# An encoder block on one core: sum of q or k first in a unit's side work, and feed-forward values without the token's scale

## The chip, the cores and the metric

The kernel runs on one core of one Trainium2 chip. The metric is the device time of one launch in microseconds (us), lower is better. Before the change it is 940.92 us, the median of three runs that lie between 940.85 and 941.05.

The core's engines are named as in its profile: PE (TensorE, matrix products), PEld (the loading of PE's weights, which overlaps with PE), DVE (VectorE), ACT (ScalarE), POOL (GpSimd) and SP (SyncE, which here only issues DMA transfers). Each takes its instructions in the order in which the program gives them. SBUF is the core's main on-chip memory, PSUM the memory that PE writes its sums to.

## The reference, cut to what matters

One encoder layer on 256 tokens of width 2048, all in float32. `D_FF` is 5504 (43 tiles of 128), there are 12 query heads of width 128 in 4 groups of three that share one key and value head.

```python
h = rmsnorm(x, norm1_g)                      # x / sqrt(mean(x*x) + EPS) * g, per token
q, k, v, u = split(h @ w_in)                 # widths 1536, 512, 512, 512
# window attention, per query head:
scores = q @ k.T * HEAD_DIM**-0.5 - slope * abs(t - s)      # only |t - s| <= 128
m = max(scores.max(-1), sink)
p = exp(scores - m); p = p / (p.sum(-1) + exp(sink - m))
a = rmsnorm(p @ v, attn_out_g)
f = rmsnorm(real(fft2(u per group)) @ w_fourier, fourier_out_g)
x = x + concat(a, f) @ w_out
h = rmsnorm(x, norm2_g)
gate, val = split(h @ w_up)                  # 5504 columns each
gate = conv over 3 tokens, per column, + dw_b
x = x + (gelu(gate) * val) @ w_down
y = rmsnorm(x, normf_g)
```

Each token's norm is one number for the token (the scale, `1/sqrt(mean + EPS)`) and one per column (`g`). The scale of a token can therefore be applied behind a product with a weight matrix as well as ahead of it.

## The kernel before

**Two halves of a float32.** PE multiplies in a rounded form of float32 (`fp32r`). Each operand is kept as a `hi` half (rounded, a copy on ACT) and a `lo` half (what the rounding lost, a subtraction on DVE), and a product is the sum of three: hi by hi, hi by lo, lo by hi. So all weights are split on the way: `split` (lines 174 to 184) takes a raw weight tile of 128 x 2048 (1 MB), ACT writes `hi` (L181), DVE writes `lo` (L182). A split costs each of them about two microseconds.

**Units.** The work up to the feed-forward part is a row of 40 units, each with one such weight tile: 0 to 3 for u, 4 to 7 for v, 8 to 23 for k and q (`QK_ORDER`: a key head, then its three query heads, four times over), 24 to 39 for the output projection. Raw tiles are loaded on SP's queue three units ahead, in a ring of three; they are split two units ahead. A unit (`unit`) runs in this order: the list `before` of that unit (matmuls of other work), its own matmuls (`still_weights`, recorded as L350), the list `beside`, then `step` with the split of the unit two later, then the list `behind`. The order of all instructions is written out by these lists; no scheduler moves anything. So the order within `beside` is the order in which ACT, DVE, POOL and SP meet the pieces of work.

**The head work.** Attention is laid beside the matmuls of the q and k units and of the first eight output units. A query head whose unit is n passes through these stages:

- n+1, `qk_out`: ACT copies one half of the PSUM sum (L631), DVE adds the other half (L633), for a key also times the token's scale. Then `qk_parts` makes the two halves: ACT `hi`, DVE `lo`, for a query at L269 and L270 (in `split_scaled`), for a key at L643 and L644.
- n+2, `scores` (six matmuls, L654, in `before`, so ahead of the unit's own) and `scores_out`: two DVE instructions add the distance term and take the maxima `mx` (L670), and two tiny POOL instructions on 128 x 2 make `neg` from them (L674, L675). In `behind`, after the split, `exps`: two exponentials on ACT with `neg` as the bias (L684), one for the sink (L688), a tiny POOL sum.
- n+3, `weigh`: reciprocal and two DVE multiplications (L697). For heads 0 to 9 (`FLIPS`) `flip_out` follows: a 32 by 32 transpose on DVE (L314) and four DMAs on SP. Heads 10 and 11 are turned by PE one unit later instead (`turn`, `turn_out`: ACT L716, DVE L717).
- n+4, `flip_in`: one DMA on SP. n+6, `flip_parts`: the halves of the turned weights, two ACT (L739) and two DVE (L740) instructions.
- n+7 (for heads 10 and 11 n+5), `values` (six matmuls, L749, in `before`) and `values_out`, which squares the result on ACT (L486), makes its halves (L269, L270) and adds the squares up on POOL (L490).

In any one q unit, several heads are thus under way, each at another stage. The order within `beside` is set in the loop over `i` below `slot_of`: `flip_parts`, `weigh` with `flip_out`, `flip_in`, `qk_out`, `values_out`, `turn_out`, `scores_out`, `qk_parts`, and after these the split.

**The feed-forward part.** 43 gate tiles and 43 value tiles, each one weight tile; `scaled_sum` copies one half of the PSUM sum (ACT, L922), adds the other (DVE, L924) and multiplies by `r2b`, the token's scale spread over all partitions (DVE, L925). The gate goes through the convolution (`gate_conv`) and GELU, then `val_mult` multiplies it with the value tile. The down-projection of the first 36 tiles is done in five groups by a scheme with seven products in place of eight for a matrix of two by two blocks (`product` items); their results are added onto `xs`, the residual stream x, by `product_out` (L1122) as they come, or held in PSUM or in `Z` and added at the end by `shared_out`. Tiles 36 to 39 (`LATE`) and 40 to 42 (`LAST`) are multiplied plainly; `last_post` adds the last of them and starts the squares of the final norm, with `EPS` added for the first piece (lines 1170 to 1172).

Of the kernel before, what the change touches and what calls it, by code (L numbers as in the profile page):

```python
# [8 lines left out]
F32 = mybir.dt.float32  # L9
F32R = mybir.dt.float32r  # L10
AF = mybir.ActivationFunctionType
ALU = mybir.AluOpType

P = 128
D = 2048
# [11 lines left out]
EPS = 1e-6  # L27
# [28 lines left out]
FLIPS = range(NH - 2)  # L56
# [48 lines left out]
def block_kernel(  # L105
# [19 lines left out]
    nc = tc.nc  # L125
    SL = slopes()
    ctx.enter_context(tc.manual_schedule())
    base = ctx.enter_context(tc.tile_pool(name="base", bufs=1))
# [131 lines left out]
    ps = bank(dn, "ps_warm")  # L260
# [13 lines left out]
    def rstd_of(ssq, width, name, n=2, r=None):  # L274

        var = base.tile([P, n], F32, tag="var" + name, name="var" + name)
        nc.vector.tensor_scalar(var, ssq, 1.0 / width, EPS, ALU.mult, ALU.add)
        if r is None:
            r = base.tile([P, n], F32, tag="rstd" + name, name="rstd" + name)
        nc.gpsimd.tensor_tensor(r, var, half_pow[:, 0:n], ALU.pow)  # L280
        return r
# [7 lines left out]
    def spread(r, dst, name):  # L289

        t = wp.tile([P, 512], F32, tag="junk", name=f"diag{name}")
        dgs = [t[:, b * P : (b + 1) * P] for b in range(2)]
        for b, dg in enumerate(dgs):
            nc.vector.tensor_scalar(dg, ident, r[:, b : b + 1], None, ALU.mult)
        ps = bank(dn, "ps_spread" + name)
        for b in range(2):
            nc.tensor.matmul(
                ps[:, b * P : (b + 1) * P], ones, dgs[b], start=True, stop=True
            )
        nc.vector.tensor_copy(dst, ps[:, :S])  # L300
# [72 lines left out]
    before, beside, behind = {}, {}, {}  # L373

    def at(when, i, f, *a):
        when.setdefault(i, []).append((f, a))
# [13 lines left out]
    for c in range(4):  # L390
        t = base.tile([P, 4, 512], F32R, tag=f"hT{c}", name=f"hT{c}")
# [234 lines left out]
    qk_sb, st = {}, {}  # L626
    sq_a = ph.tile([P, S], F32, tag="sq", name="sq_a")

    def qk_out(kind, h, ps):
        tmp = ph.tile([P, S], F32, tag="tmp", name=f"tmp_{kind}{h}", bufs=2)  # L630
        nc.scalar.activation(tmp, ps[:, S : 2 * S], AF.Copy)  # L631
        add = ph.tile([P, S], F32, tag="add", name=f"add_{kind}{h}", bufs=2)
        nc.vector.tensor_tensor(add, ps[:, 0:S], tmp, ALU.add)  # L633
        if kind == "k":
            nc.vector.tensor_tensor(add, add, r1b, ALU.mult)
        st["add", kind, h] = add
# [125 lines left out]
    for i in range(N_QK, N_OUT + 8):  # L762
        heads = {i - s: h for (kind, h), s in slot_of.items() if kind == "q"}
        new = [kh for kh, s in slot_of.items() if i - s == 1]
        for n, h in sorted(heads.items()):
            if n == 5 + 2 * (h in FLIPS):
                at(before, i, values, h)
        if 4 in heads and heads[4] not in FLIPS:
            at(before, i, turn, heads[4])
        if 2 in heads:  # L770
            at(before, i, scores, heads[2])
        if 6 in heads and heads[6] in FLIPS:
            at(beside, i, flip_parts, heads[6])
        if 3 in heads:
            at(beside, i, weigh, heads[3])
            if heads[3] in FLIPS:
                at(beside, i, flip_out, heads[3])
        if 4 in heads and heads[4] in FLIPS:
            at(beside, i, flip_in, heads[4])
        for kind, h in new:  # L780
            at(beside, i, lambda k=kind, h=h: qk_out(k, h, st.pop(("ps", k, h))))
        for n, h in sorted(heads.items()):
            if n == 5 + 2 * (h in FLIPS):
                at(beside, i, values_out, h)
        if 4 in heads and heads[4] not in FLIPS:
            at(beside, i, turn_out, heads[4])
        if 2 in heads:
            at(beside, i, scores_out, heads[2])
        for kind, h in new:
            at(beside, i, qk_parts, kind, h)  # L790
        if 2 in heads:
            at(behind, i, exps, heads[2])

# [126 lines left out]
    def scaled_sum(ps, name):  # L920
        tmp = fp.tile([P, S], F32, tag="ftmp", name=f"ft_{name}")
        nc.scalar.activation(tmp, ps[:, S : 2 * S], AF.Copy)  # L922
        add = fp.tile([P, S], F32, tag="fadd", name=f"fa_{name}", bufs=3)
        nc.vector.tensor_tensor(add, ps[:, 0:S], tmp, ALU.add)  # L924
        nc.vector.tensor_tensor(add, add, r2b, ALU.mult)  # L925
        sums_of[name] = add

    def gate_conv(j):
# [182 lines left out]
    def product_out(g, c, p, ps):  # L1111
        tt = nc.vector.tensor_tensor
        if p in ("P6", "P7"):
            z = Z[c, p]
            if g == 0:
                nc.scalar.activation(z, ps, AF.Copy)
            else:
                tt(z, ps, z, ALU.add)
        else:
            n, t = {"P2": (0, 0), "N3": (1, 0), "N4": (0, 1)}[p]  # L1120
            xb = xs[2 * n + c][:, t, :]
            tt(xb, ps, xb, ALU.add)  # L1122

    def shared_out(c, step):

        p1, n5, u, p7 = held[c, "P1"], held[c, "N5"], Z[c, "P6"], Z[c, "P7"]
        x00, x10, x01, x11 = (xs[2 * n + c][:, t, :] for n in range(2) for t in range(2))
        tt = nc.vector.tensor_tensor
        if step == 0:
            tt(u, p1, u, ALU.add)  # L1130
            tt(x00, p1, x00, ALU.add)
            w = st["w", c] = wp.tile([P, 512], F32, tag="junk", name=f"sum01_{c}")
            tt(w, n5, u, ALU.subtract)
        elif step == 1:
            tt(u, u, p7, ALU.add)
            tt(x01, x01, st["w", c], ALU.add)
            tt(x10, x10, u, ALU.add)
        else:
            w = st.pop(("w", c))
            tt(w, w, p7, ALU.subtract)  # L1140
            tt(x11, x11, w, ALU.add)

    def by_parts(ps, o, hi, lo, n, first, last):

# [14 lines left out]
    def last_post(c, b, ps, o=0, n=512):  # L1159

        xb = xs[c][:, b, o : o + n]
        nc.vector.tensor_tensor(xb, ps, xb, ALU.add)
        if c == 3:
            return
        junk = wp.tile([P, 512], F32, tag="junk", name=f"junkc{c}{b}")
        nc.scalar.activation(
            junk, xb, AF.Square, scale=D**-0.5, accum_out=ssq3[:, b, c : c + 1]
        )
        if c == 0:
            nc.vector.tensor_scalar(  # L1170
                ssq3[:, b, 3:4], ssq3[:, b, 0:1], EPS, None, ALU.add
            )
        if (c, b) == (1, 1):
            nc.gpsimd.tensor_tensor(
                ssq3[:, b, 3:4], ssq3[:, b, 3:4], ssq3[:, b, 1:2], ALU.add
            )
        if (c, b) not in ((1, 1), (2, 1)):
            nc.gpsimd.tensor_tensor(xb, xb, gfb[:, c * 512 : (c + 1) * 512], ALU.mult)
# [44 lines left out]
        still_weights(hi, lo, ps, range(12, NK))  # L1223
    tot2 = base.tile([P, 2], F32, tag="tot2", name="tot2")
    nc.vector.tensor_reduce(tot2, ssq2, mybir.AxisListType.X, ALU.add)
    spread(rstd_of(tot2, D, "2"), r2b, "2")
    ff_step(1)
    up_posts(1, *items[0], pair[0][0])
    up_posts(2, *items[1], pair[1][0])
# [208 lines left out]
```

## Time and profile before

The profiled execution took 941.03 us on the device; its span, from the first to the last recorded instruction, is 938.9 us. The mean granted clock of TensorE was 0.997 of full speed.

| engine | busy us | share of the span | instructions |
|---|---|---|---|
| PE | 928.0 | 99% | 5005 |
| PEld | 803.5 | 86% | 5005 |
| DVE | 765.5 | 82% | 945 |
| ACT | 539.6 | 57% | 672 |
| POOL | 72.9 | 8% | 104 |

The DMA queues moved 223.25 MB, 238 GB/s on average. The head work lies between about 70 and 200 us of the span, the feed-forward part from about 250 us to the end.

How to read the rows: a row of the order of time begins with its start (us from the start of the span) and its duration, then engine, line, operation, what it writes and reads, shapes, and the count of equal instructions that follow on one another; in brackets the idle time ahead of it and the instruction that ended it. A row of a group begins with the line, has the count behind an x, and then the group's busy time in us and the mean of one in ns. `lo<-raw,hi` is the DVE part of a split and thus marks the pace of the units. PE's busy share stands near 99% because a matmul's record is pipelined with the next one's; where PE waits, its next row says for how long and for what.

### The profile page before, as it was taken

The page shows a single profiled execution, that of the slowest core. Times are in us where ns is not written, and L with a number is a line of the kernel's source. Part 1 is how long each engine was busy: PE and PEld are TensorE (multiplying, and loading weights), DVE is VectorE, ACT ScalarE, POOL GpSimd, SP SyncE. Part 2 cuts the span into 40 slices and gives each one's busy share as a digit, 9 for nine tenths or more (in the row PEclk, how much of TensorE's full clock was granted, in tenths as well). Part 3 has the DMA queues.
Part 4 walks back from the last instruction along what each step waited for, and adds up shares of the span by engine and source line. Part 5 has one row for each costly group of instructions (what it writes and reads, how often), then busy time and mean ns, then how long its engine had stood idle before and what let it go on. Part 6 is the DMA issues. An engine that isn't in the chain of part 4 may idle for free.

```text
span 938.9 us, 12849 instructions
## 1 busy us (share of the span) xinstructions
PE 928.0 (99%) x5005; PEld 803.5 (86%) x5005; DVE 765.5 (82%) x945; ACT 539.6 (57%) x672; POOL 72.9 (8%) x104
## 2 busy tenths in 40 slices
PE   9999999999999999999999999999999999999996
PEld 7888888888888888888888888888888888888885
DVE  7657888778677777798888997878979789989986
ACT  7755666645554555566555665556655556655553
POOL 0102222300000000000000000000000000000002
PEclk9999999999999999999999999999999999999998
DMA  9965767557757668887797778777787978779652
GB/s 367 309 224 169 231 196 236 193 174 281 243 221 232 177 227 238 278 269 239 220 296 252 246 216 286 237 262 232 260 248 240 309 224 269 241 233 273 194 179 90
DMA packets 55148, 223.25 MB, mean 238 GB/s; under 512 B 21136, under 2 KB 25744, under 8 KB 31536
## 3 DMA queue, kind: packets, MB, share of 16 engines
q1 hardware_dynamic: 50544, 192.94, 56.8%
q0 software_dynamic: 4544, 29.49, 16.9%
q8 instruction: 39, 0.64, 0.3%
q14 instruction: 21, 0.17, 0.1%
HBM read 216.13 MB, written 6.29 MB: 237 GB/s over the span
## 4 chain that ended last, share of the span: by engine, by line
PE 95%; DVE 2%; ACT 1%; issue 1%; DMA 0%; POOL 0%; DVEq 0%; POOLq 0%; ACTq 0%
PE ps_val L350 25%; PE ps_gate L350 25%; PE ps_q L350 5%; PE ps_P L1148 3%; PE ps_P L1149 3%; PE ps_P L1147 3%; PE ps_N L1148 3%; PE ps_N L1149 3%; PE ps_N L1147 3%; PE ps_k L350 2%; PE ps_a L333 2%; PE ps_a L335 2%; PE ps_a L334 2%; PE ps_s L654 1%; PE ps_ff L333 1%; PE ps_ff L335 1%
## 5 line engine op out<-in xcount | busy, mean ns | idle before, releaser
L182 DVE TENSOR_TENSOR lo<-raw,hi 128x2048 fp32r<-128x2048 f32 (+1 forms) x129 | 293.5, 2275 | 53.9 <-ACT hi L181 53.6
L181 ACT ACTIVATE hi<-raw 128x2048 fp32r<-128x2048 f32 (+1 forms) x129 | 245.3, 1902 | 36.7 <-PE ps_a L334 14.6
L350 PE MATMUL ps_val<-hU,hi 128*128 128x512 f32 x688 | 236.2, 389 | 0.0
L350 PE MATMUL ps_gate<-hU,hi 128*128 128x512 f32 x688 | 236.2, 389 | 0.0
L350 PE MATMUL ps_val<-hU,lo 128*128 128x256 f32 x688 | 189.9, 276 | 0.0
L350 PE MATMUL ps_gate<-hU,lo 128*128 128x256 f32 x688 | 189.9, 276 | 0.0
L350 PEld LDWEIGHTS ps_gate<-hU,hi 128*128 128x128 f32 x688 | 129.1, 188 | 26.8
L350 PEld LDWEIGHTS ps_val<-hU,hi 128*128 128x128 f32 x688 | 129.1, 188 | 26.8
L350 PEld LDWEIGHTS ps_gate<-hU,lo 128*128 128x128 f32 x688 | 129.1, 188 | 1.3
L350 PEld LDWEIGHTS ps_val<-hU,lo 128*128 128x128 f32 x688 | 129.1, 188 | 1.3
L922 ACT ACTIVATE ft_g<-ps_gate 128x256 f32<-128x256 f32 x43 | 16.5, 384 | 123.0 <-PE ps_gate L350 123.0
L922 ACT ACTIVATE ft_v<-ps_val 128x256 f32<-128x256 f32 x43 | 16.5, 384 | 91.5 <-PE ps_val L350 91.5
L350 PE MATMUL ps_q<-hT,hi 128*128 128x512 f32 x192 | 65.1, 391 | 0.0
L1147 PE MATMUL ps_P<-hi_P,op_P 128*128 128x512 f32 x144 | 56.0, 389 | 0.0
L1148 PE MATMUL ps_P<-hi_P,op_P 128*128 128x512 f32 x144 | 56.0, 389 | 0.0
L1149 PE MATMUL ps_P<-lo_P,op_P 128*128 128x512 f32 x144 | 56.0, 389 | 0.0
L350 PE MATMUL ps_q<-hT,lo 128*128 128x256 f32 x192 | 51.2, 277 | 0.0
L1039 DVE TENSOR_TENSOR lo_N<-sumw,hi_N 128x2048 fp32r<-128x2048 f32 (+1 forms) x20 | 41.5, 2077 | 9.4 <-ACT hi_N L1038 9.2
L1147 PE MATMUL ps_N<-hi_N,op_N 128*128 128x512 f32 x108 | 42.0, 389 | 0.0
L1148 PE MATMUL ps_N<-hi_N,op_N 128*128 128x512 f32 x108 | 42.0, 389 | 0.0
L1149 PE MATMUL ps_N<-lo_N,op_N 128*128 128x512 f32 x108 | 42.0, 389 | 0.0
L350 PEld LDWEIGHTS ps_q<-hT,hi 128*128 128x128 f32 x192 | 35.2, 188 | 6.6
(389 smaller groups left out, 1598.9 us busy)
## 6 DMA issues: line engine op xcount, KB each, us to landing
raw<-in_w_up SPq DMA_DIRECT2D x86, 1024.0 KB, 5.6
raw<-in_w_in SPq DMA_DIRECT2D x20, 1024.0 KB, 5.3
raw<-in_w_out SPq DMA_DIRECT2D x16, 1024.0 KB, 4.9
sumw<-in_w_down POOLq DMA_DIRECT2D x16, 1024.0 KB, 8.7
raw<-in_w_down_late SPq DMA_DIRECT2D x4, 1024.0 KB, 7.0
raw<-in_w_down_last SPq DMA_DIRECT2D x4, 768.0 KB, 4.2
turnp<-flip SPq DMA_DIRECT2D x40, 64.0 KB, 2.9
flop<-turnp SPq DMA_DIRECT2D x10, 256.0 KB, 4.7
```

Of the source, the lines that this page charges most:

```text
L181: nc.scalar.activation(hi[:, 0:n], raw[:, 0:n], AF.Copy)
L182: nc.vector.tensor_tensor(lo[:, 0:n], raw[:, 0:n], f32(hi[:, 0:n]), ALU.subtract)
L333: nc.tensor.matmul(ps, ah, wh, start=first and q == q0, stop=False)
L334: nc.tensor.matmul(ps, al, wh, start=False, stop=False)
L335: nc.tensor.matmul(ps, ah, wl, start=False, stop=last and q == q0 + len(kk) - 1)
L350: nc.tensor.matmul(ps[:, x], (hi, lo)[i][:, k * P : (k + 1) * P], hk(k)[:, x], start=n == 0 and k == 0, stop=n == len(order) - 1 and k == ...
L654: nc.tensor.matmul(ps[:, b * S : (b + 1) * S], qT[:, qo + b * P : qo + (b + 1) * P], kT[:, ko : ko + S], start=n == 0, stop=n == 2,)
L922: nc.scalar.activation(tmp, ps[:, S : 2 * S], AF.Copy)
L1039: nc.vector.tensor_tensor(lo, src, f32(hi), ALU.subtract)
L1147: nc.tensor.matmul(ps, o[:, 0, p, :], hi[:, s], start=first and p == 0, stop=False)
L1148: nc.tensor.matmul(ps, o[:, 1, p, :], hi[:, s], start=False, stop=False)
L1149: nc.tensor.matmul(ps, o[:, 0, p, :], lo[:, s], start=False, stop=last and p == n - 1)
```

## The change

Four things are done.

1. In the loop that fills the lists, the order within `beside` becomes: `qk_out`, `flip_parts`, `qk_parts`, `values_out`, `weigh` with `flip_out`, `flip_in` or `turn_out`, `scores_out`. The sum of q or k, which stood in the middle, now comes first; the parts of q or k, which stood last, come third; `scores_out` now stands last, directly ahead of the split.
2. `scaled_sum` multiplies by the token's scale for gate tiles only. The value tiles stay without it, so what the down-projection adds up is too large by `1/scale` per token.
3. To match, x is divided by the token's scale before the down-projection's results are added onto it: `rms2` is the reciprocal of the scale, and the first addition onto each block of `xs` becomes `x * rms2 + value` in one instruction with a scalar per partition (in `product_out` for the first group, in `shared_out` for the block that is only touched there).
4. The final norm then works on x divided by the scale. It is the same if its `EPS` is divided by the square of the scale: `eps3 = EPS * rms2 * rms2` takes the place of `EPS` in `last_post`. `rms2` and `eps3` are two new tiles of 128 x 2 in the pool `base`, made once by three DVE instructions.

```diff
@@ the loop over i that fills the lists
+        for kind, h in new:
+            at(beside, i, lambda k=kind, h=h: qk_out(k, h, st.pop(("ps", k, h))))
         if 6 in heads and heads[6] in FLIPS:
             at(beside, i, flip_parts, heads[6])
+        for kind, h in new:
+            at(beside, i, qk_parts, kind, h)
+        for n, h in sorted(heads.items()):
+            if n == 5 + 2 * (h in FLIPS):
+                at(beside, i, values_out, h)
         if 3 in heads:
             at(beside, i, weigh, heads[3])
             if heads[3] in FLIPS:
                 at(beside, i, flip_out, heads[3])
-        if 4 in heads and heads[4] in FLIPS:
-            at(beside, i, flip_in, heads[4])
-        for kind, h in new:
-            at(beside, i, lambda k=kind, h=h: qk_out(k, h, st.pop(("ps", k, h))))
-        for n, h in sorted(heads.items()):
-            if n == 5 + 2 * (h in FLIPS):
-                at(beside, i, values_out, h)
-        if 4 in heads and heads[4] not in FLIPS:
-            at(beside, i, turn_out, heads[4])
+        if 4 in heads:
+            at(beside, i, flip_in if heads[4] in FLIPS else turn_out, heads[4])
         if 2 in heads:
             at(beside, i, scores_out, heads[2])
-        for kind, h in new:
-            at(beside, i, qk_parts, kind, h)
         if 2 in heads:
             at(behind, i, exps, heads[2])
@@ scaled_sum
-        nc.vector.tensor_tensor(add, add, r2b, ALU.mult)
+        if name[0] == "g":
+            nc.vector.tensor_tensor(add, add, r2b, ALU.mult)
@@ product_out
-            tt(xb, ps, xb, ALU.add)
+            if g == 0:
+                nc.vector.scalar_tensor_tensor(xb, xb, rms2[:, t : t + 1], ps, ALU.mult, ALU.add)
+            else:
+                tt(xb, ps, xb, ALU.add)
@@ shared_out
-            tt(x11, x11, w, ALU.add)
+            nc.vector.scalar_tensor_tensor(x11, x11, rms2[:, 1:2], w, ALU.mult, ALU.add)
@@ last_post
-                ssq3[:, b, 3:4], ssq3[:, b, 0:1], EPS, None, ALU.add
+                ssq3[:, b, 3:4], ssq3[:, b, 0:1], eps3[:, b : b + 1], None, ALU.add
@@ ahead of the feed-forward items
-    spread(rstd_of(tot2, D, "2"), r2b, "2")
+    r2 = rstd_of(tot2, D, "2")
+    spread(r2, r2b, "2")
+    rms2 = base.tile([P, 2], F32, tag="rms2", name="rms2")
+    eps3 = base.tile([P, 2], F32, tag="eps3", name="eps3")
+    nc.vector.reciprocal(rms2, r2)
+    nc.vector.tensor_tensor(eps3, rms2, rms2, ALU.mult)
+    nc.vector.tensor_scalar(eps3, eps3, EPS, None, ALU.mult)
```

## The prediction

> **What bounds the kernel now.** I read the stretches of the span first, then PE's order of time where the head work runs, then DVE, POOL and ACT in the same place. In the stretches (time, PE busy, PEld, DVE, ACT, POOL, clock, DMA share, GB/s) the feed-forward part is one unbroken run of matmuls.
>
> ```profile
> 264.00:845.00 581.00, 581.00 (x3197) 505.70 (x3196) 493.93 (x533) 335.57 (x347) 23.54 (x28) 1.00 0.78 247
> ```
>
> PE is busy 581.00 of 581.00 us and DVE leaves 87 us idle. What DVE saves there shortens nothing. Now PE in order of time: the last matmuls of a q unit, the scores, the next unit.
>
> ```profile
> 77.14 0.40 PE L350 MATMUL ps_q<-hT,lo 128*128 128x256 f32 x2
> ...
> 78.09 0.40 PE L350 MATMUL ps_k<-hT,hi 128*128 128x512 f32 x1
> ...
> 95.44 0.40 PE L350 MATMUL ps_q<-hT,lo 128*128 128x256 f32 x2
> ...
> 96.78 0.39 PE L350 MATMUL ps_q<-hT,hi 128*128 128x512 f32 x1
> ...
> 122.00 0.40 PE L350 MATMUL ps_q<-hT,lo 128*128 128x256 f32 x2
> ...
> 123.97 0.40 PE L350 MATMUL ps_q<-hT,hi 128*128 128x512 f32 x1
> ...
> 149.18 0.40 PE L350 MATMUL ps_q<-hT,lo 128*128 128x256 f32 x2
> ...
> 151.47 0.39 PE L350 MATMUL ps_q<-hT,hi 128*128 128x512 f32 x1
> ```
>
> From the first row to the last an undisturbed passage takes 0.95 us (77.14 to 78.09). The others take 1.34, 1.97 and 2.29: PE loses 0.39, 1.02 and 1.34, together 2.75 us, waiting for the parts of q. That is all the first edit can win. The three places are heads 3, 6 and 9; I call them s3, s6 and s9.
>
> Why is q late? DVE's splits (L182) mark one unit each:
>
> ```profile
> 90.97 2.29 DVE L182 TENSOR_TENSOR lo<-raw,hi 128x2048 fp32r<-128x2048 f32 x1 [1.26 <-ACT hi L181]
> ...
> 95.71 0.42 DVE L270 SCALAR_TENSOR_TENSOR qT<-add_q,qT 128x256 fp32r<-128x256 f32 x1 [0.48 <-ACT qT L269]
> ...
> 117.93 2.29 DVE L182 TENSOR_TENSOR lo<-raw,hi 128x2048 fp32r<-128x2048 f32 x1 [0.87 <-ACT hi L181]
> ...
> 124.72 2.29 DVE L182 TENSOR_TENSOR lo<-raw,hi 128x2048 fp32r<-128x2048 f32 x1 [1.38 <-ACT hi L181]
> ...
> 130.31 2.29 DVE L182 TENSOR_TENSOR lo<-raw,hi 128x2048 fp32r<-128x2048 f32 x1 [1.27 <-ACT hi L181]
> ...
> 137.63 2.29 DVE L182 TENSOR_TENSOR lo<-raw,hi 128x2048 fp32r<-128x2048 f32 x1 [0.88 <-ACT hi L181]
> 139.84 0.75 DVE L740 TENSOR_TENSOR pt<-flop,pt 128x256 fp32r<-128x256 f32 x2
> ...
> 140.70 0.90 DVE L697 TENSOR_SCALAR sc<-sc,ex 128x256 f32<-128x256 f32 x2
> ...
> 145.41 2.29 DVE L182 TENSOR_TENSOR lo<-raw,hi 128x2048 fp32r<-128x2048 f32 x1 [0.87 <-ACT hi L181]
> ...
> 149.54 0.38 DVE L633 TENSOR_TENSOR add_q<-ps_q,tmp_q 128x256 f32<-128x256 f32 x1
> ...
> 150.40 0.42 DVE L270 SCALAR_TENSOR_TENSOR qT<-add_q,qT 128x256 fp32r<-128x256 f32 x1
> ```
>
> Four units (6.79, 5.59, 7.32, 7.78) make a group of 27.48 us, as long as PE takes from s6 to s9 (123.97 to 151.47: 27.50, of which 1.34 is the wait). So this loop of DVE and ACT sets the pace here, not PE. In each unit DVE waits about 0.9 to 1.4 us for ACT's hi half, because ACT waits for the sum of q or k first.
>
> **The change part by part.** *The order of side work.* The sum comes ahead of the weighting and the stream transpose, so ACT's hi half starts sooner and that wait shrinks. But q's or k's lo half no longer stands between the scores' maxima and the split. In before, one unit late in the stage already has no q or k work and so has the new order:
>
> ```profile
> 144.28 0.31 POOL L674 TENSOR_TENSOR neg<-mx,rq_neg 128x2 f32<-128x2 f32 x1 [3.09 <-DVE mx L670]
> ...
> 165.11 2.29 DVE L182 TENSOR_TENSOR lo<-raw,hi 128x2048 fp32r<-128x2048 f32 x1 [0.88 <-ACT hi L181]
> ...
> 166.34 0.71 ACT L739 ACTIVATE pt<-flop 128x256 fp32r<-128x256 f32 x2
> 166.95 0.36 ACT L486 ACTIVATE sq<-ps_o 128x256 f32<-128x256 f32 x1
> ...
> 168.73 0.62 DVE L697 TENSOR_SCALAR sc<-sc,ex 128x256 f32<-128x256 f32 x2
> ...
> 170.34 2.29 DVE L182 TENSOR_TENSOR lo<-raw,hi 128x2048 fp32r<-128x2048 f32 x1
> ...
> 170.50 2.18 POOL L674 TENSOR_TENSOR neg<-mx,rq_neg 128x2 f32<-128x2 f32 x1 [2.17 <-DVE mx L670]
> ...
> 173.10 0.60 ACT L684 ACTIVATE sc<-sc,neg,rq_pos 128x256 f32<-128x256 f32 x1 [3.61 <-POOL neg L675]
> ...
> 174.47 0.36 ACT L486 ACTIVATE sq<-ps_o 128x256 f32<-128x256 f32 x1
> 174.73 0.46 ACT L269 ACTIVATE cat<-ps_o,vec 128x256 fp32r<-128x256 f32 x1
> 175.09 0.58 ACT L716 ACTIVATE pt<-ps_t 128x512 fp32r<-128x512 f32 x1
> ```
>
> The split starts at 170.34, POOL's tiny `neg` at 170.50, and `neg` takes 2.18 us instead of 0.31: it ends with the split (172.63, 172.68). The exponentials start 2.76 us after the split's start, and ACT's next work 1.37 us later. The Trainium skill, page "SBUF — State Buffer", section "Who interferes with whom", says that a VectorE op with two SBUF inputs and a GpSimd op that reads SBUF exclude each other, the first holding on to its end; the trace agrees (2.18 against 0.31 us). Without that rule the sum would be the first rival's 938.2, with it the forecast.
>
> ACT is in order: behind the held exponentials are the copy of the next q's PSUM half (0.36) and so the sum, now first on DVE. In a unit whose split holds `neg`, the sum starts at 2.76 + 1.37 + 0.36 + 0.03 = 4.52 us after the split, where the split alone would let it start at 2.21 (137.63 to 139.84).
>
> The four units of a group in the new order:
> - First (no scores; `neg` held): sum at 4.52; then ACT's hi of q 0.42 later (as 149.54 to its start), and on ACT 0.32, 0.26 (174.47 to 174.73), 0.36 (174.73 to 175.09), 1.93 for the split's hi: 7.81, before 6.79. The 0.42, 0.32 and 1.93 are from these ACT rows:
>
> ```profile
> 149.96 0.42 ACT L269 ACTIVATE qT<-add_q 128x256 fp32r<-128x256 f32 x1 [2.33 <-DVE add_q L633]
> 150.28 1.90 ACT L181 ACTIVATE hi<-raw 128x2048 fp32r<-128x2048 f32 x1
> ```
>
> - Second (no exponentials pending): 2.21 + 0.42 + 0.32 + 1.93 = 4.88, before 5.59. DVE is done with the scores before ACT's half, so `neg` gets through.
> - Third: DVE's work alone, 7.32 less its wait 0.88 and less 0.27 (L697 takes 0.90 where POOL's sum of squares gets in its way, else 0.62): 6.17.
> - Fourth (`neg` held): 7.78 less 0.87 and 0.27 is 6.64, plus the late start 4.52 - 2.21: 8.95, before 7.78.
>
> Sum 27.81: a group is 0.33 us longer, not shorter. For the group from 90.97 to 117.93 (26.96) the same steps give about 0.2 more.
>
> Delays against before, at PE: s3's lo half of q comes at 4.52 + 0.86 = 5.38 after its split, in before at 4.74 (90.97 to 95.71): 0.64. At s6 0.2 + 0.39 (5.38 against 4.99, 145.41 to 150.40) = 0.6; at s9 0.33 more, 0.9. Then the unit from 165.11 to 170.34, 5.23 before, gets its `neg` held too: by ACT's order 4.13 (2.76 + 1.37) + 0.61 for the two flips (166.34 to 166.95) + 0.26 + 0.36 + 1.93 = 7.3. The three units ahead of it give -0.84 + 0.71 in all (7.81 + 4.88 + 6.17 against 19.70): the split at 170.34 is 0.2 + 0.33 - 0.84 + 2.07 = 1.8 late. Its unit ends in the parts for head 10, which were ready under half a microsecond ahead of PE:
>
> ```profile
> 176.38 0.67 DVE L717 TENSOR_TENSOR pt<-ps_t,pt 128x512 fp32r<-128x512 f32 x1
> ...
> 177.39 0.40 PE L749 MATMUL ps_o<-pt,v_hi 128*128 128x256 f32 x2
> ```
>
> That takes off 0.45 (177.05 against the second matmul, 177.50): 1.3 us. The units were laid without the 0.02 to 0.05 us of every handover that the old order hid; at some ten in the held units I add 0.4. The stage costs 1.7. On SP the loads and transposes keep their order; the transposes are issued later or earlier by at most these delays.
>
> *Feed-forward values.* 43 multiplications of 0.425 us go from DVE (18.3 us). Cover: PE's unbroken run above; worth 0. If PE did wait for DVE there, it would win at most those 18.3.
>
> ```profile
> L925 DVE TENSOR_TENSOR fa_v<-fa_v,r2b 128x256 f32<-128x256 f32 x43 | 18.3, 425 | 1.5
> L1122 DVE TENSOR_TENSOR xs<-ps_N,xs 128x512 f32<-128x512 f32 x18 | 12.3, 684 | 0.0
> L811 DVE SCALAR_TENSOR_TENSOR xs<-ps_ff,rstdf,xs 128x512 f32<-128x512 f32 x8 | 5.6, 739 | 0.0
> ```
>
> *x divided by the scale, EPS in the final norm.* Three DVE ops on 128x2 once, at most 0.5 us in all, hidden by the same run; six adds of the first product group become the form with a scalar (739 against 684 ns: 0.06 each, hidden); two more late, one of them on DVE's last busy stretch: 0 to 0.1, I take 0.1. The tail's EPS operand costs nothing.
>
> Sum: 1.7 + 0.1 = 1.8 us. The profiled execution took 941.03 (span 938.9, 2.1 around it) and becomes 942.8; the median 940.92 is 0.11 lower, so 942.7. Its own range is 941.4 (half the delay) to 944.0.
>
> **The rivals.** *All waits go (faster).* If DVE still waited for ACT's half by over 0.7 us after the maxima, `neg` would pass ahead of each split, as at 144.28. Then the groups follow PE, and all 2.75 go: 940.92 - 2.75 + 0.1 = 938.2. For it: in before it passes, as at 144.28. Against: they pass because another op stands there, and the hi half comes sooner now.
>
> *The third unit is held too.* Its start would be 2.31 later, over two groups and the last: up to 6.9, 949.6; one such unit gives 945. Against: ACT's half is the later one in the second unit (4.88 against about 4.2).
>
> *Placement.* The two new tiles push every later tile 64 bytes on while the hidden state stays (in the two programs as built). If that slowed each 512-column matmul from 389 to 393 ns, the slowest such row, 1376 + 256 of them cost 6.5: 949.2.
>
> ```profile
> L350 PE MATMUL ps_val<-hU,hi 128*128 128x512 f32 x688 | 236.2, 389 | 0.0
> L333 PE MATMUL ps_ff<-hi,cat 128*128 128x512 f32 x32 | 12.6, 393 | 0.0
> ```
>
> *Nothing moves.* Gains in the second and third unit cancel the held ones: 940.9.
>
> **How the numbers follow.** Forecast 0.65, all waits go 0.13, third unit held 0.07, placement 0.05, nothing moves 0.10. From no change a measurement can tell about 0.2%, 1.9 us: 942.8 upwards is slower. The forecast lies on that edge, so I give 0.34 of it to slower and 0.31 to same. Faster 0.13, same 0.31 + 0.10 = 0.41, slower 0.34 + 0.07 + 0.05 = 0.46. The range 938.1 to 945.0 takes in the forecast's own and the rival that is faster, and leaves out the two costliest.
>
> **What would show it.** Right: about half of the `neg` rows near 2.2 us, splits that follow the maxima with no wait, waits of PE at s3, s6 and s9 of 1.0 to 2, a new one at head 10's values, and 581 of 581 in the feed-forward part. Wrong: `neg` at 0.3 throughout and no PE wait, or matmuls of 393 ns.

## The result and the profile after

The changed kernel takes 955.66 us (median of four runs, 955.35 to 955.95) against 940.98 us before: a ratio of 1.0152, with a 95% interval of 1.014 to 1.0165. It is 14.7 us slower. The forecast was 942.7 us, slower by 1.8, with a range up to 945.0.

The first view is the table of groups of the changed kernel: line, operation, count, then busy time in us and the mean of one in ns. The last row is from the same table of the kernel before.

```profile
L350 PE MATMUL ps_val<-hU,hi 128*128 128x512 f32 x688 | 240.6, 392 | 0.0
...
L350 PE MATMUL ps_val<-hU,lo 128*128 128x256 f32 x688 | 192.4, 280 | 0.0
...
L1149 PE MATMUL ps_P<-hi_P,op_P 128*128 128x512 f32 x144 | 57.1, 397 | 0.0
L1151 PE MATMUL ps_P<-lo_P,op_P 128*128 128x512 f32 x144 | 56.5, 392 | 0.0
L1150 PE MATMUL ps_P<-hi_P,op_P 128*128 128x512 f32 x144 | 55.8, 387 | 0.0
```

```profile
L350 PE MATMUL ps_val<-hU,lo 128*128 128x256 f32 x688 | 189.9, 276 | 0.0
```

The same number of the same matmuls has become slower: 392 ns where the row quoted in the prediction has 389, 280 where it was 276, and the three kinds in the products are 397, 392 and 387 instead of 389 each. A few ns sound like little, but matmuls follow one another without a gap. The stretch of 581 us that is all PE, in the view of stretches, says what it comes to. Before, it held 3197 matmuls. After:

```profile
264.00:845.00 581.00, 581.00 (x3142) 503.24 (x3141) 466.88 (x486) 330.13 (x341) 23.28 (x27) 1.00 0.77 241
```

The granted clock is 1.00 in both, PE is busy from end to end in both, and DVE has less to do than before (466.88 us instead of 493.93). Yet a matmul takes 581/3142 = 184.9 ns on average where it took 581/3197 = 181.7. The order of time shows the whole stretch, first in the kernel before, then in the changed one: the first gate matmul and the last of the value tiles.

```profile
251.30 0.39 PE L350 MATMUL ps_gate<-hU,hi 128*128 128x512 f32 x1
...
891.81 0.28 PE L350 MATMUL ps_val<-hU,lo 128*128 128x256 f32 x1
```

```profile
254.70 0.39 PE L350 MATMUL ps_gate<-hU,hi 128*128 128x512 f32 x1
...
907.11 0.28 PE L350 MATMUL ps_val<-hU,lo 128*128 128x256 f32 x1
```

Between these two marks lie 640.5 us before and 652.4 after: 11.9 us of the loss arise here, where the change took work away. 3.4 us had arisen by the first gate matmul (251.30 to 254.70). That is the part where the order of side work was changed, but its matmuls may have become slower as well. For that part the view of POOL in order of time:

```profile
119.65 2.18 POOL L674 TENSOR_TENSOR neg<-mx,rq_neg 128x2 f32<-128x2 f32 x1 [2.21 <-DVE mx L670]
131.79 0.20 POOL L674 TENSOR_TENSOR neg<-mx,rq_neg 128x2 f32<-128x2 f32 x1 [5.83 <-DVE mx L670]
138.77 2.18 POOL L674 TENSOR_TENSOR neg<-mx,rq_neg 128x2 f32<-128x2 f32 x1 [2.23 <-DVE mx L670]
147.83 2.18 POOL L674 TENSOR_TENSOR neg<-mx,rq_neg 128x2 f32<-128x2 f32 x1 [2.22 <-DVE mx L670]
```

In this stretch two `neg` of the three in each group of four units are now held for 2.18 us, as the prediction's account of the new order has it. So there are two causes to tell apart, and the larger one is not the one I forecast.

### The profile page after: what moved, and what is told of

Same layout as the page of the kernel before. It is cut to its first block, busy times and chain, and to the rows that moved or that the text cites. A ratio compares the mean times of both kernels' runs of the same rounds, so it can differ in the third digit from the quotient of the medians.

```text
span 954.2 us, 12810 instructions
## 1 busy us (share of the span) xinstructions
PE 942.6 (99%) x5005; PEld 812.4 (85%) x5005; DVE 746.8 (78%) x905; ACT 540.6 (57%) x672; POOL 80.7 (8%) x104
## 3 DMA queue, kind: packets, MB, share of 16 engines
HBM read 216.13 MB, written 6.29 MB: 233 GB/s over the span
## 4 chain that ended last, share of the span: by engine, by line
PE 85%; DVE 5%; ACT 4%; issue 3%; POOL 2%; DMA 0%; DVEq 0%; POOLq 0%; ACTq 0%
PE ps_gate L350 25%; PE ps_val L350 25%; PE ps_P L1149 4%; PE ps_P L1151 3%; PE ps_P L1150 3%; PE ps_N L1149 3%; PE ps_N L1151 3%; PE ps_N L1150 3%; PE ps_a L335 2%; PE ps_a L333 2%; PE ps_a L334 2%; POOL neg L674 2%; ACT hi L181 1%; ACT sc L684 1%; PE ps_ff L333 1%
## 5 line engine op out<-in xcount | busy, mean ns | idle before, releaser
L181 ACT ACTIVATE hi<-raw 128x2048 fp32r<-128x2048 f32 (+1 forms) x129 | 245.3, 1902 | 36.4 <-PE ps_a L334 14.9
L350 PE MATMUL ps_val<-hU,hi 128*128 128x512 f32 x688 | 240.6, 392 | 0.0
L350 PE MATMUL ps_gate<-hU,hi 128*128 128x512 f32 x688 | 240.6, 392 | 0.0
L350 PE MATMUL ps_gate<-hU,lo 128*128 128x256 f32 x688 | 192.4, 280 | 0.0
L350 PE MATMUL ps_val<-hU,lo 128*128 128x256 f32 x688 | 192.4, 280 | 0.0
```

The lines of the kernel that those rows point to most:

```text
L181: nc.scalar.activation(hi[:, 0:n], raw[:, 0:n], AF.Copy)
L350: nc.tensor.matmul(ps[:, x], (hi, lo)[i][:, k * P : (k + 1) * P], hk(k)[:, x], start=n == 0 and k == 0, stop=n == len(order) - 1 and k == ...
```

## The experiments

Theory P: the two new tiles, which take 32 bytes of each partition apiece, and not the arithmetic they serve, cost some 12 us, since they move all later tiles 64 bytes on and the matmuls run slower there. Theory H: the rest, 2 to 3 us, is POOL's held `neg` in the new order. Rival O: PE is slowed by something in the order or the arithmetic of the side work.

### Moving the tiles without the change, and the change without moving the tiles

```diff
# kernel before, two new tiles (four in the second kernel)
     spread(rstd_of(tot2, D, "2"), r2b, "2")
+    for q in range(2):
+        pad = base.tile([P, 2], F32, tag=f"pad{q}", name=f"pad{q}")
+        nc.vector.memset(pad, 0.0)
# changed kernel, no new tiles
-    rms2 = base.tile([P, 2], F32, tag="rms2", name="rms2")
-    eps3 = base.tile([P, 2], F32, tag="eps3", name="eps3")
+    rms2, eps3 = ssq3[:, 0, 8:10], ssq3[:, 0, 10:12]
```

> The kernel before plus two 32-byte tiles, set to zero once and never read, at the place where the change has its two new tiles; order and arithmetic as before. Theory P (the 64 bytes by which all later tiles move slow the matmuls down): 512-column gate and value matmuls follow one another in 229.4 ns instead of 226.8, the 256-column ones in 117.2 instead of 113.3, and the time is 941.0 + about 13.8 = 954.8. Rival O (the order or the arithmetic of the side work slows PE, through what ACT and DVE read and write beside it): no more than the two memsets, 941.0.

> The changed kernel, all its edits kept, but with its two small values in unused columns of the tile ssq3, so that no tile moves. Theory P: matmuls at 226.8 and 113.3 ns again; what is left is the order's own cost, in the trace after 0.16 + 0.31 us more wait ahead of the scores of heads 3 and 9 and 0.46 ahead of head 10's values, so 941.0 + 0.9 to 941.0 + 1.8 (my forecast): 941.9 to 942.8; the held POOL rows stay near 2.18 us. Rival O: 955, as after.

> The kernel before plus four 32-byte tiles (128 bytes). If what counts under theory P is the position within 128 bytes: 941.0 and the matmuls at 226.8 and 113.3 ns. If any move away from the old place costs (a distance to another tile): 945 to 956. Rival O: 941.0 as well, so this run speaks only if the one with 64 bytes is slow.

Measured, beside 941.18 us for the kernel before on the same chip: 953.57 with 64 bytes of padding (1.013, 1.0116 to 1.0144), 943.73 for the change without new tiles (1.0028, 1.0018 to 1.0039), 959.24 with 128 bytes (1.0191, 1.0178 to 1.0205). The stretch of 581 us of the first (padding only) and of the second (all edits, no tile moved):

```profile
264.00:845.00 581.00, 581.00 (x3142) 503.03 (x3141) 484.37 (x526) 329.73 (x342) 23.28 (x27) 1.00 0.77 243
```

```profile
264.00:845.00 581.00, 581.00 (x3201) 505.93 (x3200) 476.22 (x493) 335.27 (x346) 23.27 (x27) 1.00 0.78 246
```

3142 matmuls with nothing but padding, as in the changed kernel; 3201 with every edit but no moved tile, about as before (3197). That is rival O's end. 12.4 us come from where the tiles stand, 2.5 from the edits, together 14.9 against the 14.7 measured. The executions of the kernel without new tiles lie between 943.02 and 944.87, so the 2.5 is good to about half a microsecond. With padding alone the first gate matmul starts at 251.90 us, so that of the 3.4 us that had arisen there 0.6 belong to the moved tiles. 128 bytes are worse than 64, and worse than either range that I had given them, so the place within 128 bytes is not what counts.

### Which edit costs the 2.5 us

The first kernel is the one before with the new list of `beside` and nothing else; the second has all the edits of the feed-forward part, the old order, and no new tiles.

> The kernel before with only the new order of the side work; no new tiles. My account puts all that is left of the loss without the moved tiles on the order: 941.2 + 2.2 to 2.5, so about 943.5, with the waits of the run without new tiles (1.90, 2.24 and 2.87 us ahead of heads 3, 6 and 9, 0.46 ahead of head 10's values). If the values' edit were to blame instead: 941.2 or, with the waits gone, 938.5.

> The changed kernel with the old order of the side work, its two small values in unused columns of ssq3. It leaves out the multiplications of the value tiles and scales x instead. My account: 941.2 + 0.0 to 0.3 (nothing saved, since PE does not wait for DVE in the feed-forward part; at most a delay in the tail). If the 18.3 us that DVE saves reached PE anywhere: under 940.

The order alone takes 943.51 us (1.0026, 1.0017 to 1.0035), the values alone 941.05 (0.9997, 0.9988 to 1.0006), beside 941.24. So the 18.3 us of DVE are worth nothing measurable, and the order costs what was left, 2.3 us (its executions lie between 942.72 and 944.46). Its waits, in the changed kernel without new tiles (PE in order of time):

```profile
95.20 0.40 PE L350 MATMUL ps_q<-hT,lo 128*128 128x256 f32 x2
96.18 1.20 PE L654 MATMUL ps_s<-kT,qT 128*128 128x256 f32 x6 [0.58 <-ACT qT L269]
97.21 0.62 PE L350 MATMUL ps_q<-hT,hi 128*128 128x512 f32 x2
...
122.41 0.40 PE L350 MATMUL ps_q<-hT,lo 128*128 128x256 f32 x2
...
124.76 0.62 PE L350 MATMUL ps_q<-hT,hi 128*128 128x512 f32 x2
...
149.94 0.40 PE L350 MATMUL ps_q<-hT,lo 128*128 128x256 f32 x2
151.89 1.20 PE L654 MATMUL ps_s<-kT,qT 128*128 128x256 f32 x6 [1.55 <-ACT qT L269]
152.93 0.62 PE L350 MATMUL ps_q<-hT,hi 128*128 128x512 f32 x2
...
179.59 0.39 PE L749 MATMUL ps_o<-pt,v_hi 128*128 128x256 f32 x1 [0.46 <-DVE pt L717]
```

The passage ahead of head 3 takes 97.21 - 95.20 = 2.01 us instead of 1.34, the one ahead of head 6 2.35 instead of 1.97, the one ahead of head 9 2.99 instead of 2.29, and there is a new wait of 0.46 at head 10's values.

### Taking the small instruction off POOL

```diff
# changed kernel without new tiles
-        nc.gpsimd.tensor_tensor(neg, mx, rq_neg, ALU.mult)
-        nc.gpsimd.tensor_scalar(neg, neg, sink_neg[:, h : h + 1], None, ALU.min)
+        nc.vector.tensor_tensor(neg, mx, rq_neg, ALU.mult)
+        nc.vector.tensor_scalar(neg, neg, sink_neg[:, h : h + 1], None, ALU.min)
# changed kernel without new tiles, neg on POOL: qk_parts behind scores_out again
         for kind, h in new:
             at(beside, i, lambda k=kind, h=h: qk_out(k, h, st.pop(("ps", k, h))))
...
-        for kind, h in new:
-            at(beside, i, qk_parts, kind, h)
...
             at(beside, i, scores_out, heads[2])
+        for kind, h in new:
+            at(beside, i, qk_parts, kind, h)
```

> The changed kernel without new tiles, with the two tiny instructions that make neg moved from POOL to DVE, ahead of the split; new order kept. If the held POOL instruction is what makes the new order slow: the exponentials no longer start 2.76 us behind the split's start, the waits ahead of heads 3, 6 and 9 shrink below those of before (0.39, 1.02, 1.34) and the time is between 938.2 and 940.5. If the order is slow for another reason (ACT's or DVE's own sequence, the transposes started later): 943 to 944, as without the new tiles.

> The changed kernel without new tiles, with the parts of q or k put back to the last place, between the maxima and the split; the sum of q or k stays first. If a DVE instruction between the maxima and the split is enough to let POOL's neg pass: neg near 0.31 us again, and the time 938.2 to 940.5. If neg is still held where ACT's hi half is ready early: 941 to 943.

> The kernel before, old order, with only the two instructions that make neg moved from POOL to DVE. In before they pass in eleven of twelve cases, so if the 2.9 us that this move won together with the new order came from the pair, here it is about 0: two DVE instructions of 0.16 and 0.23 us more in each unit with scores, against a shorter way to the exponentials; 940.5 to 941.8. If the move alone wins: 938 to 939.

With `neg` on DVE the new order takes 938.37 us against 941.24 (0.9971, 0.996 to 0.9982): 2.9 us faster than the kernel before, and the fastest of all. With the parts of q last and `neg` on POOL it is 940.26 (0.9991, 0.9982 to 1.0). With `neg` on DVE in the old order (the first two edits above, made in the kernel before) it is 941.52 against 941.60 (1.0001, 0.9992 to 1.001). So neither the new order nor the move pays by itself; together they do. PE in the fastest kernel, at the places of heads 3 and 9:

```profile
95.74 0.40 PE L350 MATMUL ps_q<-hT,lo 128*128 128x256 f32 x2
95.97 0.88 PE L654 MATMUL ps_s<-kT,qT 128*128 128x256 f32 x6
96.69 0.63 PE L350 MATMUL ps_q<-hT,hi 128*128 128x512 f32 x2
...
148.07 0.40 PE L350 MATMUL ps_q<-hT,lo 128*128 128x256 f32 x2
148.31 0.88 PE L654 MATMUL ps_s<-kT,qT 128*128 128x256 f32 x6
149.02 0.63 PE L350 MATMUL ps_q<-hT,hi 128*128 128x512 f32 x2
```

Both passages take the undisturbed 0.95 us, and so does the one ahead of head 6 (121.91 to 122.86). All 2.75 us of waiting are gone, which is what the prediction's first rival priced at 938.2. In the kernel with the parts last, the first of POOL's two instructions passes in eleven of twelve units, and in six of these the second is held in its place, by a split that starts between the two (here at 134.25):

```profile
134.07 0.31 POOL L674 TENSOR_TENSOR neg<-mx,rq_neg 128x2 f32<-128x2 f32 x1 [2.11 <-DVE mx L670]
134.48 2.20 POOL L675 TENSOR_SCALAR neg<-neg,sink_neg 128x2 f32<-128x2 f32 x1
```

### Why moved tiles slow the matmuls

Five kernels move different tiles by different distances, which are those of the built programs. The hidden state, as the prediction calls it, is the tiles `hT`, named `hU` in the feed-forward part: the operand of a gate, value, q or k matmul whose columns PE multiplies with the weights. `shifts` says by how many elements of 4 bytes the hi and the lo half of a unit's weights start behind the start of their buffers (`SHIFT` is 16), and `PRODUCT_SHIFT` does so for the products.

```diff
# less192: kernel before, all later tiles 192 bytes back
-    ssq3 = base.tile([P, 2, 32], F32, tag="ssq3", name="ssq3")
+    ssq3 = base.tile([P, 2, 8], F32, tag="ssq3", name="ssq3")
# halves_moved: kernel before, hi and lo of all weights 64 bytes (16 elements) on, no tile moved
-    shifts = [(SHIFT, SHIFT)] * 8 + [(0, SHIFT)] * 16 + [(0, 0)] * 16
+    shifts = [(32, 32)] * 8 + [(16, 32)] * 16 + [(16, 16)] * 16
...
-PRODUCT_SHIFT = 28
+PRODUCT_SHIFT = 44
# all_moved: kernel before, the padding ahead of the hidden state
+    for q in range(2):
+        pad = base.tile([P, 2], F32, tag=f"pad{q}", name=f"pad{q}")
+        nc.vector.memset(pad, 0.0)
     for c in range(4):
         t = base.tile([P, 4, 512], F32R, tag=f"hT{c}", name=f"hT{c}")
# state_moved: the same, and ssq3 64 bytes shorter, so that only the hidden state and ssq3 move
# shifts_swapped: changed kernel
+    shifts = [(0, 0)] * 8 + [(SHIFT, 0)] * 16 + [(SHIFT, SHIFT)] * 16
...
+PRODUCT_SHIFT = 12
```

> The changed kernel with its two new tiles where they are, but the 64-byte shifts inside the weight buffers exchanged (hi half shifted instead of lo in the q, k, gate and value units, none instead of both for u and v, both instead of none for the plain products, 12 instead of 28 elements for the other products), so that every weight half stands within 128 bytes where it stood before. Theory P with the position of the weight halves within 128 bytes as its cause: gate and value matmuls at 226.8 and 113.3 ns, which wins 86 x 16 x (2.6 + 3.9) ns = 8.9 us of the loss and 1.7 in the q and k units: about 945, and 942 to 943 if the products are cured too (their stationary operands stay moved). If it is another tile's position: 955.

> The kernel before with ssq3 192 bytes shorter (its unused columns), so that all later tiles move back by 192 bytes; that is the same place within 256 bytes as 64 bytes further on. If a position within 256 bytes decides: gate and value matmuls at 229.7 and 117.1 ns and the first product line at 235.8, as with 64 bytes of padding, 953 to 954. If it does not: other intervals, and a time anywhere from 941 to 960.

> The kernel before with no tile moved, only the hi and lo halves of all weights 64 bytes further on inside their buffers. If the place of the weight halves is what slows the gate and value matmuls: 229.5 and 117.2 ns there, 86 x 16 x 6.5 ns = 8.9 us and 1.7 in the q and k units, so 951 or more; the products, whose other operand stays, may change either way. If it is another tile: 941.

> The kernel before with the 64 bytes of padding ahead of the hidden state, so that the hidden state and all later tiles move together and keep their distances. If the distance between the two operands of a matmul decides: gate, value, q and k matmuls at 226.8 and 113.3 ns, and a time between 941 (all) and 944.5 (the products slow by 3 us as in after). If the place itself decides: about 953.

> The kernel before with the hidden state alone 64 bytes further on (and ssq3 64 bytes shorter, so that the weights and all later tiles stay). Distance theory: gate, value, q and k matmuls slow, products at 226.7 ns as before, 950 to 953. Place of the weights alone: 941.

| kernel | what stands elsewhere | us | ratio to before, interval |
|---|---|---|---|
| shifts_swapped | all later tiles +64, weight halves as before within 128 bytes | 963.85 | 1.024, 1.0221 to 1.0259 |
| less192 | all later tiles -192 | 953.62 | 1.0132, 1.0117 to 1.0147 |
| halves_moved | weight halves alone +64 | 955.50 | 1.0154, 1.0139 to 1.0169 |
| all_moved | hidden state and all later tiles +64 | 957.08 | 1.0168, 1.0151 to 1.0185 |
| state_moved | hidden state (and ssq3) alone +64 | 955.90 | 1.0158, 1.0143 to 1.0174 |

Minus 192 bytes give the same as plus 64, down to the groups: 392, 280, and 396 for the first product line, 953.6 us both. A place within 256 bytes as what counts fits this pair; no second pair was tried. My expectation for the swapped shifts (945) was wrong: they restore the place within 128 bytes only. Moving the weight halves alone or the hidden state alone costs at least as much as moving one against the other by padding. (For the hidden state I had expected 950 to 953; it is more because the products slow down too.) That speaks for the distance between the two operands of a matmul. But then the kernel that moves both together should have been fast, and it was the slowest of these four. Its order of time (PE) shows why it is not a plain case of place:

```profile
262.25 0.39 PE L350 MATMUL ps_gate<-hU,hi 128*128 128x512 f32 x1
262.47 0.28 PE L350 MATMUL ps_gate<-hU,lo 128*128 128x256 f32 x1
262.59 0.39 PE L350 MATMUL ps_val<-hU,hi 128*128 128x512 f32 x1
...
263.95 0.61 PE L297 MATMUL ps_spread<-diag,ones 128*128 128x128 f32 x4
264.32 0.48 PE L350 MATMUL ps_gate<-hU,hi 128*128 128x512 f32 x1
...
265.45 0.40 PE L350 MATMUL ps_gate<-hU,hi 128*128 128x512 f32 x1
265.68 0.28 PE L350 MATMUL ps_gate<-hU,lo 128*128 128x256 f32 x1
265.80 0.40 PE L350 MATMUL ps_gate<-hU,hi 128*128 128x512 f32 x1
```

A pair of 512 and 256 columns takes 0.34 us up to 263.95 (262.25 to 262.59), the fast rhythm of the kernel before. The q and k matmuls ahead of it, whose operands moved together too, also keep the times of the kernel before (391 ns for the 512 columns of q, where padding alone has 394). Then four small matmuls of another kind interrupt the run, and from there a pair takes 0.35 us (265.45 to 265.80), in every gate and value tile up to the one that starts at 854 us; behind the first of the plain products, which comes next, it is fast again. The same instructions, with operands at the same places within 256 bytes, run in two rhythms. Inside a gate or value tile of the slow stretch, from its second pair on, the intervals of one kind differ by no more than 1 ns, while DVE and ACT start and end their own instructions beside them; that speaks against these two as the cause. To see whether the interruption chooses, I added twenty more, of 1 to 305 columns:

```diff
             ps = bank(mm, f"ps_{kind}{j}")
+            if kind == "gate" and j >= 3 and j % 2:
+                w = 1 + 16 * ((j - 3) // 2)
+                nc.tensor.matmul(ps[:, 0:w], ones, hT[0][:, 0, 0:w].bitcast(F32), start=True, stop=True)
             still_weights(*halves.pop(up_index[n]), ps, range(NK))
```

> The kernel with the hidden state and all later tiles moved together (957.1 us), with one useless product of 1, 17, 33, ... 321 columns ahead of every second gate tile, which interrupts the unbroken run of matmuls twenty times; its result is overwritten. Phase theory (with the distances kept the fast rhythm exists, and how the run is entered decides which rhythm it keeps until the next interruption): the interval pair of 232 and 118 ns changes at some of the interruptions, to 226 and 114 in some stretches, and the time is several us below 957 + the interruptions' own cost (20 x about 0.3 us). Place theory: 232 and 118 in every stretch, about 963.

> The kernel before with the same twenty useless products. Phase theory: some stretches fall into the slow rhythm (232 and 118 ns or the like), and the time lies well above 941 + 6. Place theory: 226.8 and 113.3 ns in every stretch, 943 to 947.

> The changed kernel with the same twenty useless products. If with the changed distances no fast rhythm exists: 229.5 and 117.2 ns or slower in every stretch, 957 to 962. If the phase alone decides: some stretches at 226.8 and 113.3 ns.

With both operands moved together, the interruptions made the kernel faster, 953.45 us (1.0126, 1.0097 to 1.0155) instead of 957.08, although they take 6.3 us themselves (by the starts of the matmuls: the useless products and the longer first interval behind each). In the kernel before they cost 10.9 us, 952.51 (1.0116, 1.0086 to 1.0145): 6.5 us are their own time, and the rest comes with the slow rhythm, in 23 of its 84 undivided gate and value tiles. The changed kernel went to 963.11 (1.0228, 1.0199 to 1.0258), 7.4 us more, of which 6.2 are their own time; I had expected 962 at most. In the first of the three, three of the interruptions (the useless product is the row with 1, with 49 and with 65 columns):

```profile
286.45 0.28 PE L1248 MATMUL ps_gate<-hU,ones 128*128 128x1 f32 x2
...
363.34 0.32 PE L1248 MATMUL ps_gate<-hU,ones 128*128 128x49 f32 x2
...
364.61 0.40 PE L350 MATMUL ps_gate<-hU,hi 128*128 128x512 f32 x1
364.84 0.28 PE L350 MATMUL ps_gate<-hU,lo 128*128 128x256 f32 x1
364.96 0.40 PE L350 MATMUL ps_gate<-hU,hi 128*128 128x512 f32 x1
...
391.51 0.33 PE L1248 MATMUL ps_gate<-hU,ones 128*128 128x65 f32 x2
...
393.11 0.39 PE L350 MATMUL ps_gate<-hU,hi 128*128 128x512 f32 x1
393.34 0.28 PE L350 MATMUL ps_gate<-hU,lo 128*128 128x256 f32 x1
393.45 0.39 PE L350 MATMUL ps_gate<-hU,hi 128*128 128x512 f32 x1
```

The first, a single column, turns the slow rhythm into the fast one (intervals of 233 and 117 ns before it, 227 and 113 behind). Behind the one with 49 columns a pair takes 0.35 us, behind the one with 65 columns 0.34, and between two interruptions the rhythm of the tiles changes nowhere but at the plain products. Read from the starts of all gate and value matmuls, the medians are 226 to 227 and 113 to 114 ns in the fast rhythm, 232 to 233 and 117 to 118 in the slow one; the kernel before with interruptions has both as well (slow for the first time at 573 us). The changed kernel with interruptions has 229 to 231 and 117 in every one of its stretches: with its distance between weights and hidden state there is no fast rhythm to fall into.

So two things decide in these runs. The distance between a matmul's operands decides whether a fast rhythm exists: at the old distance it does, at 64 bytes more it was seen in no stretch. Where it exists, the way in which a run of matmuls begins behind an interruption decides whether the run has it, for hundreds of microseconds. What in the chip makes the two rhythms was not measured; that PE's two reads, of the weights for the next matmul and of the columns for this one, get in each other's way in one phase and not in another fits the runs, but is only argued. The Trainium skill, page "SBUF — State Buffer", section "Who interferes with whom", calls PE's two read ports independent and says that PE waits for nobody. No run here shows a wait at a port; that a move of 64 bytes makes 392 ns of 389 is nothing that the section would lead one to expect. What the same section says of VectorE and GpSimd, as the prediction tells it, agrees with the rows shown here (2.18 us behind the start of a split, 0.20 without).

## Why the prediction was wrong

**The step that failed: the price and the chance of the rival on placement.** I had noted that the two tiles push every later tile 64 bytes on while the hidden state stays, and that this could slow matmuls. I priced it by the slowest 512-column row that the trace showed, 393 instead of 389 ns, at 6.5 us, and gave it 0.05. What it cost is 12.4 us. 392 ns for the 512-column gate and value matmuls was close; what I left out are the 256-column ones, 280 instead of 276, and the products, up to 397. By group means, 86 tiles of 16 pairs at 3 + 4 ns are 9.6 us, and the products, 252 of each of three kinds (144 in P, 108 in N), lose 397 + 392 + 387 - 3 x 389 = 9 ns a triple, 2.3 us: together 11.9 of the 12.4. (Durations of matmuls that overlap are not what they add to the time. By the starts, from the first gate to the last value matmul of the kernel with padding alone, the pairs lose 9.1 us and the products 2.9, which makes the 11.9 of that stretch.) The row that I took as the upper bound stands in a kernel whose long run of matmuls is in its fast rhythm throughout; it could not bound a rhythm that the kernel did not contain. The sum had the placement at nothing, and 942.7 could only come true with that.

**The new order of side work.** Mechanism right, term somewhat too small: 1.7 forecast, 2.3 measured (943.51 against 941.24). In the run without new tiles the steps can be checked one by one against DVE's row of time:

```profile
118.27 2.29 DVE L182 TENSOR_TENSOR lo<-raw,hi 128x2048 fp32r<-128x2048 f32 x1
122.79 0.42 DVE L633 TENSOR_TENSOR add_q<-ps_q,tmp_q 128x256 f32<-128x256 f32 x1 [2.23 <-ACT tmp_q L631]
126.21 2.25 DVE L182 TENSOR_TENSOR lo<-raw,hi 128x2048 fp32r<-128x2048 f32 x1
...
131.09 2.29 DVE L182 TENSOR_TENSOR lo<-raw,hi 128x2048 fp32r<-128x2048 f32 x1 [0.61 <-ACT hi L181]
...
137.38 2.29 DVE L182 TENSOR_TENSOR lo<-raw,hi 128x2048 fp32r<-128x2048 f32 x1
...
146.44 2.29 DVE L182 TENSOR_TENSOR lo<-raw,hi 128x2048 fp32r<-128x2048 f32 x1
...
165.55 2.29 DVE L182 TENSOR_TENSOR lo<-raw,hi 128x2048 fp32r<-128x2048 f32 x1
...
172.85 2.29 DVE L182 TENSOR_TENSOR lo<-raw,hi 128x2048 fp32r<-128x2048 f32 x1
```

The sum of q starts 4.52 us behind a held split (118.27 to 122.79), as worked out. The four units take 7.94, 4.88, 6.29 and 9.06, forecast 7.81, 4.88, 6.17 and 8.95; which two are held was right as well. The group is 28.17 us, not 27.81: 0.12 or so in each held unit and the third, the handovers for which I had put one term of 0.4 at the end. The longer passages make PE 0.67 us late at head 3, 1.05 at head 6 and 1.75 at head 9, forecast 0.64, 0.6 and 0.9, so that by head 9 some 0.8 more had gathered than the steps gave, against the 0.4 put down. The three units behind 146.44 take 19.11 us, forecast 18.86, and the next takes 7.30 as forecast; the 0.71 that stands beside the -0.84 in the prediction is in none of its later sums. The new wait at head 10's values came out at 0.46.

**Feed-forward values and EPS.** Worth nothing, as forecast: 941.05 against 941.24.

**The rivals.** "All waits go" did not happen in the changed kernel, but its price was right to 0.2 us: 938.37 where `neg` is off POOL. Its condition, a wait of over 0.7 us for ACT's half behind the maxima, did not come about: 0.61 us at 131.09, none at the other splits shown. What I held against it, that `neg` passes in the kernel before because another instruction stands between the maxima and the split, holds for certain only for the first of POOL's two instructions. "The third unit is held too" did not occur (0.20 us at 131.79 in the profile after). "Nothing moves" fell with the order's own run.

**What was to be seen.** Seven of the twelve `neg` near 2.2 us, splits without a wait behind most of the maxima, longer waits at heads 3, 6 and 9, a new one at head 10's values and 581 of 581 us: all there. The sign named for the placement, matmuls of 393 ns, was there too, at 392.

## What to carry to other kernels

Where a matmul stream is the bound, an edit that adds or resizes a tile is an edit of every address behind it: look at where the pools end up before and after, price a change of place by all matmuls of the stream, and put small new values into room that exists already. A tiny instruction on POOL that met a large DVE one with two inputs in SBUF was held for nearly all of it here (2.18 of 2.29 us); putting it on DVE is worth a try before an order is judged. And the removed DVE operations beside a PE that is never idle were worth nothing, though their row summed to 18.3 us.

## What the runs showed of the hardware that I had not expected

A stream of equal matmuls, with operands at equal places within 256 bytes, has a rhythm that it keeps: 226 and 113 ns or 232 and 118 ns for 512 and 256 columns, at the same granted clock. A small product between two tiles can change it, both ways, even one of a single column; without such an interruption it stayed for 595 us in the run with all tiles moved (264.32 to the end of the tile that starts at 854). A move of one operand against the other by 64 bytes took the fast rhythm away in every stretch of the changed kernel with interruptions (229 to 231 and 117 ns), and moves of -192 and +64 bytes are alike. Products slowed down even where only the hidden state moved, which they do not read: in that run's groups their three kinds take 390, 392 and 397 ns instead of 389. That they take over the rhythm of the gate and value tiles between them fits: in the run with all tiles moved and interruptions, the same products follow one another in 226 to 227 ns in the fast stretches and in about 225, 231 and 237 in the slow ones. It was not tested without such tiles.
